# Down-projection of a streaming encoder layer: 38 of 44 k-tiles by one level of Strassen's algorithm, with sums of weights formed by accumulating transfers

## The chip, the core and the metric

The kernel runs on one core of one Trainium2 chip. The metric is the device time of one execution in microseconds (us). Before the change it is 2918.61 us, the median of 3 runs (2916.6 to 2919.67). The engines are TensorE (PE; its weight loads stand apart as PEld), VectorE (DVE), ScalarE (ACT), GpSimd (POOL) and SyncE (SP). SP issues nearly all transfers (queue q1), POOL the rest (queue q0); both queues run on the core's same 16 DMA engines.

## What is computed

One layer, 512 prompt frames and 64 sample frames together, model width 2048, FFN width 5632, float32:

```python
mod = jax.nn.silu(c) @ w_ada[l] + b_ada[l]
sh1, sc1, g1, sh2, sc2, g2 = jnp.split(mod[:, None, :], N_MOD, axis=-1)
h = rmsnorm(x, norm1[l]) * (1 + sc1) + sh1
mix, s_a, s_b, s_c = token_mixers(h, ...)      # w_in, two recurrences, w_out
x = x + g1 * mix
h = rmsnorm(x, norm2[l]) * (1 + sc2) + sh2
gate, val = jnp.split(h @ w_up, 2, axis=-1)
act = jax.nn.silu(causal_dwconv(gate, st, ffn_conv_w) + ffn_conv_b) * val
x = x + g2 * (act @ w_down)                    # the changed product, 5632 x 2048
y = rmsnorm(x, final_norm)
```

## The kernel before

**Tiling.** Activations lie as [128 features, 2 halves, 288 frames]: the 576 frames are cut into two halves of 256 prompt and 32 sample frames. Float32 products are made of three float32r products: each operand is split into a high part (ACT copies it, `hi`) and a rest (DVE subtracts, `lo`), and w·x is taken as hi·hi + hi·lo + lo·hi. So a product of a 128 x 128 weight block with both halves is 6 matmuls (`mm6`, L551: L560 four times, L562 twice). Weights come in pieces of 512 KB (`wtile`, L652, and `split`, L638: SP's load, ACT's copy L648, DVE's subtraction L649).

**Stages, in order of the program.** The head loads `w_ada` and forms the modulation `mod` on PE (L752, L756, L757), turns and normalises x (`x_turn`, `x_norm`) and starts on `w_in`; then come the heads of the two recurrences beside the products with `w_in`, `w_out`, the second norm, the up-projection (`up`, L1437), the down-projection (`down`, L1480) and the last four k-tiles with the final norm (`final`, L1511).

**POOL in the head.** POOL takes the reciprocal roots of five blocks of x (`rsqrt`, L143), clears four small tiles (`nar`, L867) and one more (`wg`, L953), and then begins the small triangular inverses of the first recurrence (`inverse16`, L346): it writes a matrix to DRAM (L355), reads blocks of it back (L361) and runs 28 short operations (L370, L371). What PE does with the inverse begins at L243.

**The up-projection** is by Strassen already: 44 output tiles t with 7 products each (`up_product`, L1362; 24 matmuls of 290 columns, hi·hi, hi·lo, lo·hi on one bank after the other), and sums of weights made by DVE (L1330, L1339, L1349, L1354). `steps` runs over (t, c), and `up_prep` splits two products ahead.

**The down-projection.** `down` loads the running sum x from DRAM (`xd`, 16 tiles), and for each of ten groups of four k-tiles goes over 16 output tiles m: 4 times `mm6` into a tile of PSUM, then `residual` (L1147, two DVE operations, L1150) adds g2 times that to x1[m]. Activations are loaded from DRAM (`actd`) and split ahead (`acts`, L1468). The eleventh group is done in `final`, half by half, and normalised as it goes.

**What sets the order.** The code is written in one order, and a scheduler puts each engine's instructions in an order of its own: an operation that waits for nothing that comes earlier in the code may be moved far ahead of its place, unless it is tied. An engine executes its list strictly in that order, and an instruction that waits for a semaphore holds up all that stand behind it. `high_priority` moves weight loads ahead by some 80 places.

Of the kernel before, what the change touches and what calls it, by code (L numbers as in the profile page):

```python
# [52 lines left out]
B11, T2, T1, B21, T3, B22, T4 = range(7)  # L53

# [46 lines left out]
class Kern:  # L101
# [530 lines left out]
    def raw_late(self):  # L632

        pool, tag = self.raws[self.n_raw % N_RAW]
        self.n_raw += 1
        return pool.tile([P, 1024], F32, tag=tag, name=self.name("raw"))
# [578 lines left out]
    def put(self, c, j, src, place=None):  # L1215

        place = place or self.places.pop(0)
        t = self.slot(place, F32R)
        self.split_z(t[:, 0], t[:, 1], src)
        self.combos[c, j] = t[:, 0], t[:, 1], place  # L1220
# [216 lines left out]
    def up(self):  # L1437
# [30 lines left out]
    def acts(self, g):  # L1468

        nc, out = self.nc, []  # L1470
        places = self.sets[g % 2]
        for n in range(4):
            raw, hh, hl = [self.slot(places[3 * n + i], (F32, F32R, F32R)[i], HT) for i in range(3)]
            nc.sync.dma_start(raw, self.actd[4 * g + n])
            nc.scalar.activation(hh, raw, AF.Copy)
            nc.vector.tensor_tensor(hl, raw, hh.bitcast(F32), op=ALU.subtract)
            out.append((hh, hl))
        return out

    def down(self):  # L1480
        free = [self.combos[c, j][2] for c in range(7) for j in range(NPAIR)]
        take = lambda n: [free.pop(0) for _ in range(n)]
        self.sets = [take(12), None]
        acts = self.acts(0)
        self.raw = self.raw_late
        places = take(KD)
        self.sets[1] = take(12)
        for m in range(KD):
            self.x1[m] = self.slot(places[m], F32)
            self.nc.sync.dma_start(self.x1[m], self.xd[m])  # L1490
        for g in range(NFF // 4 - 1):
            for m0 in range(0, KD, 2):
                wh, wl = self.wtile(self.w_down(4 * g, m0))
                if m0 == 6:
                    ahead = self.acts(g + 1)
                for m in range(m0, m0 + 2):
                    ps = self.pgt()
                    c = slice((m - m0) * P, (m - m0 + 1) * P)
# [3 lines left out]
            acts = ahead  # L1502
        g = NFF // 4 - 1
        self.final(acts, free + self.sets[(g + 1) % 2] + self.sets[g % 2][0::3])
# [5 lines left out]

    def final(self, acts, free):  # L1511
# [3 lines left out]

        wide = lambda n: [free.pop(0) for _ in range(n)]
# [5 lines left out]
        for h in range(2):  # L1522
# [3 lines left out]
            for m in range(KD):  # L1526
# [6 lines left out]
                self.residual(ps[:, m % 2:m % 2 + 1], self.x1[m][:, h:h + 1], self.mod[:, 5, m])  # L1533
# [40 lines left out]
    def final_part(self, h, q, blocks):  # L1574
# [3 lines left out]
        for c0, n, y, ms in blocks:  # L1578
            ps = self.bank()
            z0 = c0 if c0 < HP else ZS  # L1580
            for j in range(4):
                T.transpose(ps[:n, j * P:(j + 1) * P], self.x1[4 * q + j][:, h, z0:z0 + n], self.c["ident"])
# [23 lines left out]
def layer_kernel(tc, i, o):  # L1606
    nc = tc.nc
    with ExitStack() as ctx:
# [14 lines left out]
        K.actd = [dp.tile([P, 2, HT], F32, name=f"actd{t}") for t in range(NFF)]  # L1623
        K.hp = pool(ctx, "hp", bufs=1)
# [138 lines left out]
```

## Time and profile before

The profiled execution took 2917.59 us, of which 2915.8 us are the span from the first to the last instruction. Its clock was 0.994 of full speed.

| stage | from to, us | PE busy | DMA share |
|---|---|---|---|
| head, up to POOL's first L355 | 0 to 204.65 | 181.3 us | 0.92, 0.84, 0.94, 0.69 in its four parts |
| recurrences, w_in, w_out, norm | 204.65 to 1311.7 | 98 to 99% | about 0.55 |
| up-projection | 1311.7 to 2331.7 | 100% (1320 to 2310) | 0.36 |
| down-projection and final | 2331.7 to 2915.8 | 100% (2360 to 2800) | 0.33 (2360 to 2800) |

Of all DMA traffic (399.84 MB), 385.82 MB go by SP's queue and 10.68 MB by POOL's. "Busy" of PE is modelled from pipelined matmuls; the pace of matmuls is better read as a stretch of time over the number of matmuls begun in it. The DMA share is the mean share of time in which the 16 DMA engines work on a packet.

### The profile page before, as it was taken

What the parts mean: (1) busy time and instruction counts of PE and PEld (TensorE: products, weight loads), DVE (VectorE), ACT (ScalarE), POOL (GpSimd) and SP (SyncE); (2) the same over time, 40 slices, a digit from 0 to 9 for tenths busy, and PEclk for the clock granted to TensorE, in tenths of its full rate; (3) what the DMA queues carried; (4) which work ended last, traced back from release to release, by engine and by line L of the source; (5) the groups of instructions that cost most, each with busy time, mean ns of one, the idle gap of its engine ahead of it and who ended that gap; (6) DMA issues with size and microseconds to landing.
All of it is one profiled execution on the core that took longest, in us unless ns stands there. A gap on an engine that the chain in (4) does not pass through costs nothing.

```text
span 2915.8 us, 52420 instructions
## 1 busy us (share of the span) xinstructions
PE 2865.9 (98%) x21052; PEld 2766.4 (95%) x21052; DVE 2133.5 (73%) x3543; ACT 1239.9 (43%) x2118; POOL 321.0 (11%) x587
## 2 busy tenths in 40 slices
PE   7999999999999999999999999999999999999998
PEld 3599999999999999999999999999999999999997
DVE  5788878777777786468887888887888855555555
ACT  6574566544433233354444444444444422222223
POOL 0015432234210001000000000000000000000000
PEclk8999999999999999999999999999999999999999
DMA  8975555555456548333333333333333553333221
GB/s 302 302 205 148 157 154 159 155 140 165 124 149 174 145 144 250 113 104 106 107 100 105 106 107 106 107 99 106 105 106 107 175 185 102 114 102 113 87 81 66
DMA packets 511879, 399.84 MB, mean 137 GB/s; under 512 B 45865, under 2 KB 437764, under 8 KB 511636
## 3 DMA queue, kind: packets, MB, share of 16 engines
q1 hardware_dynamic: 506212, 385.82, 44.5%
q0 software_dynamic: 5424, 10.68, 1.1%
q8 instruction: 166, 2.72, 0.4%
q14 instruction: 77, 0.63, 0.1%
HBM read 356.27 MB, written 40.13 MB: 136 GB/s over the span
## 4 chain that ended last, share of the span: by engine, by line
PE 90%; DVE 4%; ACT 3%; DMA 2%; issue 1%; POOL 0%; SPq 0%; ACTq 0%; DVEq 0%; POOLq 0%
PE g L560 30%; PE g L562 15%; PE g L1372 9%; PE g L1373 8%; PE g L1374 8%; PE bank L1373 3%; PE bank L1372 3%; PE bank L1374 3%; PE bank L161 1%; DVE acc L819 1%; PE bank L825 1%; PE bank L433 1%; PE bank L752 1%; DVE wl L649 1%; PE bank L756 1%
## 5 line engine op out<-in xcount | busy, mean ns | idle before, releaser
L560 PE MATMUL g<-slot,wh 128*128 128x288 f32 x3168 | 551.4, 295 | 0.2 <-DVE slot L1150 0.2
L1372 PE MATMUL g<-slot,wh 128*128 128x290 f32 x1760 | 533.6, 303 | 3.0 <-ACT p L1384 2.6
L648 ACT ACTIVATE wh<-raw 128x1024 fp32r<-128x1024 f32 x239 | 253.0, 1059 | 658.5 <-PE g L560 622.5
L1373 PE MATMUL g<-slot,wh 128*128 128x290 f32 x1760 | 525.4, 299 | 0.0
L1374 PE MATMUL g<-slot,wl 128*128 128x290 f32 x1760 | 520.6, 296 | 0.0
L560 PEld LDWEIGHTS g<-slot,wh 128*128 128x128 f32 x3168 | 464.5, 188 | 0.7 <-DVE slot L1150 0.5
L560 PE MATMUL g<-hh,wh 128*128 128x288 f32 x1984 | 449.8, 306 | 2.3 <-ACT hh L1159 1.0
L560 PE MATMUL g<-hl,wh 128*128 128x288 f32 x1984 | 431.9, 297 | 0.0
L562 PE MATMUL g<-hh,wl 128*128 128x288 f32 x1984 | 431.5, 298 | 0.0
L1150 DVE SCALAR_TENSOR_TENSOR slot<-g,mod,slot 128x512 f32<-128x512 f32 (+1 forms) x448 | 201.8, 491 | 286.9 <-PE g L562 286.0
L1319 ACT ACTIVATE wh<-raw 128x1024 fp32r<-128x1024 f32 x176 | 186.8, 1061 | 390.2 <-PE g L1373 380.0
L1372 PEld LDWEIGHTS g<-slot,wh 128*128 128x128 f32 x1760 | 331.2, 188 | 17.6 <-ACT p L1384 11.7
L562 PE MATMUL g<-slot,wl 128*128 128x288 f32 x1584 | 341.7, 294 | 0.0
L1374 PEld LDWEIGHTS g<-slot,wl 128*128 128x128 f32 x1760 | 336.5, 191 | 0.0
L1373 PEld LDWEIGHTS g<-slot,wh 128*128 128x128 f32 x1760 | 335.6, 191 | 0.1
L649 DVE TENSOR_TENSOR wl<-raw,wh 128x1024 fp32r<-128x1024 f32 x239 | 291.4, 1220 | 52.2 <-ACT wh L648 51.3
L560 PEld LDWEIGHTS g<-hh,wh 128*128 128x128 f32 x1984 | 318.6, 190 | 5.5 <-ACT hh L1159 1.3
L560 PEld LDWEIGHTS g<-hl,wh 128*128 128x128 f32 x1984 | 320.9, 189 | 0.3
L562 PEld LDWEIGHTS g<-hh,wl 128*128 128x128 f32 x1984 | 319.4, 189 | 0.2 <-issue 0.2
L562 PEld LDWEIGHTS g<-slot,wl 128*128 128x128 f32 x1584 | 255.1, 188 | 0.0
L819 DVE SCALAR_TENSOR_TENSOR acc<-xr,ct,acc 128x512 f32<-128x512 f32 x322 | 230.3, 750 | 1.7 <-DMA xr<-in_w_ada_dram 1.7
L1320 DVE TENSOR_TENSOR wl<-raw,wh 128x1024 fp32r<-128x1024 f32 x176 | 214.7, 1220 | 18.3 <-ACT wh L1319 18.1
(373 smaller groups left out, 4540.5 us busy)
## 6 DMA issues: line engine op xcount, KB each, us to landing
raw<-in_w_up_dram SPq DMA_DIRECT2D x176, 512.0 KB
raw<-in_w_in_dram SPq DMA_DIRECT2D x108, 512.0 KB
raw<-in_w_down_dram SPq DMA_DIRECT2D x88, 512.0 KB
xr<-in_w_ada_dram SPq DMA_DIRECT2D x86, 512.0 KB
ax<-in_w_ada_dram SPq DMA_DIRECT2D x42, 512.0 KB
hraw<-in_w_ada_dram SPq DMA_DIRECT2D x40, 512.0 KB
raw<-in_w_out_dram SPq DMA_DIRECT2D x32, 512.0 KB
slot<-actd SPq DMA_DIRECT2D x44, 288.0 KB
```

The source lines that it names most:

```text
L161: self.nc.tensor.transpose(ps[:, b * P:(b + 1) * P], src4[:, b], self.c["ident"])
L560: T.matmul(ps[:, h if bank is None else bank, :n], wh, x[:, h, :n], start=f, stop=False)
L562: T.matmul(ps[:, h if bank is None else bank, :n], wl, ah[:, h, :n], start=False, stop=stop)
L648: nc.scalar.activation(hi[:, :n_], raw[:, :n_], AF.Copy)
L649: nc.vector.tensor_tensor(lo[:, :n_], raw[:, :n_], hi[:, :n_].bitcast(F32), op=ALU.subtract)
L819: V.scalar_tensor_tensor(acc[s], w[:, k], col, acc[s], op0=ALU.mult, op1=ALU.add)
L1150: self.nc.vector.scalar_tensor_tensor(x1[:, :, z], ps[:, :, c], gain[:, q:q + 1], x1[:, :, z], op0=ALU.mult, op1=ALU.add)
L1319: self.nc.scalar.activation(hi, src, AF.Copy)
L1320: self.nc.vector.tensor_tensor(lo, src, hi.bitcast(F32), op=ALU.subtract)
L1372: T.matmul(ps, wh[:, j], hi, start=(c < 3 and j == 0), stop=False, skip_group_check=True)
L1373: T.matmul(ps, wh[:, j], lo, start=False, stop=False, skip_group_check=True)
L1374: T.matmul(ps, wl[:, j], hi, start=False, stop=(j == NPAIR - 1), skip_group_check=True)
```

## The change

38 of the 44 k-tiles of the down-projection (2 to 39) are taken by one level of Strassen's algorithm. They form two halves of 19 (`NDOWN`), which with the two halves of the output width and the two halves of the frames make a 2 x 2 by 2 x 2 block product. Tiles 0 and 1 (`FIRST`) are done by `mm6` ahead of it, and 40 to 43 in `final` as before. The 19 pairs of k-tiles are cut into groups of 3, 4, 4, 4 and 4, and each group goes over four quarters q of the output half, with seven products c each; a product is 18 or 24 matmuls of 288 columns.

- `down_pair` makes the seven sums of activations of a pair of k-tiles and splits each (7 ACT copies, 7 DVE subtractions, 4 DVE sums). 
- `down_out` adds a finished product into one of 16 tiles of running sums (`acc`) or 4 of a common part (`e0`); `down_finish` puts a quarter together at the end: `e0`, times g2, plus x from DRAM. In `final`, `final_sum` takes the place of `residual`.
- The sums of weights are not made by DVE. `down_sums` has POOL issue 80 transfers from DRAM to DRAM: four copies and four accumulating transfers for each of 10 pieces, 72 of them of 256 rows by 1024 floats (1.05 MB) and 8 of half that. Each accumulating transfer waits for the landing of what it adds to. The generator is advanced twice in each of the first 40 rounds of the loop of the up-projection. `down_load` then loads weights and sums of weights alike, in 512 KB (384 KB in the first group).

```diff
+    def down_sums(self):
+        dma, add = self.nc.gpsimd.dma_start, ALU.add
+        pieces = [(g, k) for g in range(len(GROUPS)) for k in range(0, GROUPS[g], 2)]
+        for batch in (pieces[:5], pieces[5:]):
+            for op in range(8):
+                for g, k in batch:
+                    rows = slice(k * P, min(k + 2, GROUPS[g]) * P)
+                    a11, a12, a21, a22 = [self.down_block(g, *at)[rows] for at in ((0, 0), (0, 1), (1, 0), (1, 1))]
+                    s1, s2, s3, s4 = [w[rows] for w in self.ws[g]]
+                    to, of = ((s1, a21), (s1, a22), (s2, s1), (s2, a11), (s3, a11), (s3, a21), (s4, s2), (s4, a12))[op]
+                    if op % 2:
+                        dma(to, of, accum_op=add)
+                    else:
+                        dma(to, of)
+                    yield
     def up(self):
...
+        sums = self.down_sums()
         for n, (t, c) in enumerate(steps):
+            if c in (1, 4):
+                next(sums, None)
...
+    def down_product(self, step, c):
...
+        for a in range(2):
+            ps = self.banks[a][(0, 1, 2, 0, 1, 2, 1)[c]]
+            f = slice(a * P, (a + 1) * P)
+            for j in range(n):
+                hi, lo, _ = self.combos[c, j0 + j]
+                T.matmul(ps, wh[:, j, f], hi, start=(c < 3 and j == 0), stop=False, skip_group_check=True)
+                T.matmul(ps, wh[:, j, f], lo, start=False, stop=False, skip_group_check=True)
+                T.matmul(ps, wl[:, j, f], hi, start=False, stop=(j == n - 1), skip_group_check=True)
...
     def down(self):
...
-        for g in range(NFF // 4 - 1):
-            for m0 in range(0, KD, 2):
-                wh, wl = self.wtile(self.w_down(4 * g, m0))
...
-                    for k in range(4):
-                        self.mm6(ps, wh[:, k, c], wl[:, k, c], acts[k], k == 0, k == 3)
-                    self.residual(ps, self.x1[m], self.mod[:, 5, m])
...
+        steps = [((g, q), c) for g in range(len(GROUPS)) for q in range(4) for c in range(7)]
...
+        for n, (step, c) in enumerate(steps):
+            g, q = step
+            self.down_prep(n + 2)
+            self.down_product(step, c)
+            self.down_out(step, c)
...
+            if g < last and (q, c) in ((2, 0), (3, 1), (3, 3), (3, 5)):
...
+                self.down_pair(j, raws.pop(j))
+                j += 1
...
+        K.ws = [[dp.tile([n * P, D // 2], F32, name=f"ws{g}{c}") for c in range(4)] for g, n in enumerate(GROUPS)]
```

**Where the 80 transfers stand.** These are POOL's rows at the start of the program before the change (nar, rs and wg are the small tiles named above, d the matrix in DRAM that the first inverse writes):

```order
L867 MEMSET nar_777 128x264
L867 MEMSET nar_1055 128x264
L143 ISA
L143 TENSOR_TENSOR rs<-rs,mhalf 128x1 x4
L143 TENSOR_TENSOR rs<-rs,mhalf 64x1
L867 MEMSET nar_1333 128x264
L867 MEMSET nar_1456 128x264
L953 MEMSET wg 64x512
L355 DMA d_385_2078<-m_1867 128x512
L361 DMA m_1727<-d_385_2078 8x16x16 x4
```

And these are POOL's rows at the same place of the changed program (ws are the sums of weights in DRAM; L1543 is the copy, L1541 the accumulating transfer; all other lines stand two further down):

```order
L869 MEMSET nar_1075 128x264
L1543 DMA ws_177<-in_w_down_dram 256x1024
L1543 DMA ws_177<-in_w_down_dram 128x1024
L1543 DMA ws_181<-in_w_down_dram 256x1024 x2
L1543 DMA ws_185<-in_w_down_dram 256x1024
L1541 DMA ws_177<-in_w_down_dram 256x1024
L1541 DMA ws_177<-in_w_down_dram 128x1024
L1541 DMA ws_181<-in_w_down_dram 256x1024 x2
L1541 DMA ws_185<-in_w_down_dram 256x1024
L145 ISA
L145 TENSOR_TENSOR rs<-rs,mhalf 128x1
L1543 DMA ws_178<-ws_177 16x16384
```

Further on, still ahead of the first inverse, POOL's list of the changed program ends the transfers so:

```order
L869 MEMSET nar_1476 128x264
L1541 DMA ws_195<-in_w_down_dram 256x1024
L1543 DMA ws_188<-ws_186 16x16384
L1543 DMA ws_192<-ws_190 16x16384 x2
L1543 DMA ws_196<-ws_194 16x16384 x2
L1541 DMA ws_188<-in_w_down_dram 256x1024
L1541 DMA ws_192<-in_w_down_dram 256x1024 x2
L1541 DMA ws_196<-in_w_down_dram 256x1024 x2
L955 MEMSET wg 64x512
L357 DMA d_385_2098<-m_1887 128x512
```

All 80 transfers have moved from the loop of the up-projection, where the code has them, to the head: 24 stand ahead of the fifth root of x (L145), 49 ahead of the third `nar`, 69 ahead of the fourth, and the last eleven ahead of `wg` and the first inverse (L357). PE's and SP's lists are the same as before up to the end of the up-projection, ACT's but for one place, and DVE's but for a row or two moved by a few places.

**DVE where one group of pairs is followed by the next.** In the down-projection before the change DVE's list repeats this (L649 splits a weight piece, L1150 adds a product to x):

```order
L649 TENSOR_TENSOR wl_26503<-raw_26501,wh_26502 128x1024
L1150 SCALAR_TENSOR_TENSOR slot_25597<-g_26387,mod,slot_25597 128x2x256
L1150 SCALAR_TENSOR_TENSOR slot_25597<-g_26387,mod,slot_25597 128x2x32
L1150 SCALAR_TENSOR_TENSOR slot_25599<-g_26414,mod,slot_25599 128x2x256
L1150 SCALAR_TENSOR_TENSOR slot_25599<-g_26414,mod,slot_25599 128x2x32
```

In the changed program it has, in the last quarter of the second group (L1557 splits a weight piece, L1599 and L1601 add a product to the running sums, L1226 splits a sum of activations, L1501, L1505 and L1509 make such sums):

```order
L1557 TENSOR_TENSOR wl_27744<-raw_27582,wh_27743 128x1024
L1226 TENSOR_TENSOR slot_27780<-raw_27679,slot_27780 128x288
L1226 TENSOR_TENSOR slot_27786<-raw_27679,slot_27786 128x288
L1226 TENSOR_TENSOR slot_27789<-t_3691_27783,slot_27789 128x288
L1601 TENSOR_TENSOR slot_25672<-g_27619,slot_25672 128x576
L1226 TENSOR_TENSOR slot_27792<-raw_27681,slot_27792 128x288
L1226 TENSOR_TENSOR slot_27796<-raw_27681,slot_27796 128x288
L1509 SCALAR_TENSOR_TENSOR raw_27681<-raw_27679,raw_27681 128x288
L1557 TENSOR_TENSOR wl_27805<-raw_27613,wh_27804 128x1024
```

The work of `down_pair` now stands among the splits, spread over the twelve products around a change of group.

More of the change, by code (lines that the diff above doesn't have):

```diff
@@ L1465, in up, with stage @@
         self.up_act(t, self.v, self.ca)
[L1468 to L1478, printed above, removed]
+    def stage(self):
+        n = self.n_stage = self.n_stage + 1
+        tag = ("v", "cb", "v", "ca")[n % 4]
+        return self.ub.tile([P, 2, HZ], F32, tag=tag, bufs=2 if tag == "v" else 1, name=self.name("raw"))[:, :, :HT]
@@ new lines, in act_load, with act_split, pair_load @@
+    def act_load(self, t):
+        raw = self.stage()
+        self.nc.sync.dma_start(raw, self.actd[t])
+        return raw
+    def act_split(self, raw):
+        hh, hl = [self.slot(self.places.pop(0), F32R, HT) for _ in range(2)]
+        self.nc.scalar.activation(hh, raw, AF.Copy)
+        self.nc.vector.tensor_tensor(hl, raw, hh.bitcast(F32), op=ALU.subtract)
+        return hh, hl
+    def pair_load(self, j):
+        return [self.act_load(FIRST + j + half * NDOWN) for half in range(2)]
@@ L1503, in down @@
-        g = NFF // 4 - 1
-        self.final(acts, free + self.sets[(g + 1) % 2] + self.sets[g % 2][0::3])
+        self.raws += [(self.ua, "s1"), (self.ua, "s2")]
+        self.places = firsts = take(2 * FIRST)
+        firsts = list(firsts)
+        acts = [self.act_split(self.act_load(k)) for k in range(FIRST)]
+        self.places = take(7 * GROUPS[0])
+        quarters = lambda places: [self.slot(p, F32, HT) for p in places]
+        self.acc = {}
+        for row in range(2):
+            for h in range(2):
+                self.acc[row, h] = quarters(take(4))
@@ new lines, in down @@
+        self.e0_places = take(4)
+        self.e0 = quarters(self.e0_places)
+        self.places += free + firsts
+        self.g2 = self.sp.tile([P, KD, 2], F32, tag="g2", bufs=1, name="g2")
+        for half, f in ((0, 1.0), (1, -1.0)):
+            A.activation(self.g2[:, 8 * half:8 * half + 8], self.mod[:, 5, 8 * half:8 * half + 8], AF.Copy, scale=f)
+        steps = [((g, q), c) for g in range(len(GROUPS)) for q in range(4) for c in range(7)]
+        self.steps = steps
+        raws = {0: self.pair_load(0)}
```

155 lines of the change are left out of this document (136 added, 19 removed).

## The prediction

> **What bounds the kernel now.** I read the page's summary and its 40 slices first, then the busy time by stretches.
>
> ```profile
> span 2915.8 us, 52420 instructions
> PE 2865.9 (98%) x21052; PEld 2766.4 (95%) x21052; DVE 2133.5 (73%) x3543; ACT 1239.9 (43%) x2118; POOL 321.0 (11%) x587
> PE   7999999999999999999999999999999999999998
> DMA  8975555555456548333333333333333553333221
> ```
>
> PE is busy nearly everywhere, so fewer matmuls shorten the kernel wherever their weights and activations come in time. The DMA row says something else: it stands at 8, 9, 7 in the first three slices (0 to 219 us) and at 3 in the long middle. The stretches (columns: us, then busy us and count of PE, PEld, DVE, ACT, POOL, then PE's granted clock, DMA share, GB/s) give it in numbers:
>
> ```profile
> 0.00:50.00 50.00, 32.97 (x138) 19.87 (x139) 17.73 (x41) 35.17 (x75) 4.52 (x13) 0.84 0.92 312
> 50.00:100.00 50.00, 47.80 (x205) 24.26 (x204) 41.20 (x62) 30.13 (x44) 0.32 (x1) 0.99 0.84 281
> 100.00:150.00 50.00, 48.37 (x235) 28.69 (x234) 39.55 (x61) 27.24 (x37) 0.32 (x1) 1.00 0.94 317
> 150.00:204.65 54.65, 52.17 (x396) 51.07 (x395) 43.47 (x103) 41.56 (x93) 0.52 (x2) 1.00 0.69 193
> 125.00:150.00 25.00, 24.14 (x109) 13.00 (x108) 19.59 (x30) 13.26 (x19) 0.00 (x0) 1.00 0.95 318
> 1320.00:2310.00 990.00, 990.00 (x7218) 975.40 (x7217) 813.57 (x1005) 442.58 (x524) 68.17 (x129) 1.00 0.36 105
> 2360.00:2800.00 440.00, 440.00 (x3329) 440.00 (x3329) 234.09 (x383) 95.94 (x105) 0.00 (x0) 1.00 0.33 103
> ```
>
> So the head is bound by PE and DMA at once: its DMA engines have 0.92 × 50 + 0.84 × 50 + 0.94 × 50 + 0.69 × 54.65 = **172.7 us** of work in 204.65 us, and never show more than 0.95. The up- and down-projection have two thirds of the DMA time free.
>
> **The change, part by part.** *Matmuls.* By the code the last stage had 44 × 16 × 6 = 4224; now it has 6 × 16 × 6 = 576 and 19 × 4 × 2 × 7 × 3 = 3192, that is 456 fewer. The down-projection begins 3329 in 440 us, one in 132.2 ns: **60.3 us** less. But the new ones come in the order of the up-projection (hi·hi, hi·lo, lo·hi, one bank after the other), which begins 7218 of 290 columns in 990 us, one in 137.2 ns; at 288 columns 136.2, so 4.0 × 3192 = **12.9 us** back. (Some of that is waits of the up-projection alone; none of it would be the lower end.)
>
> *DVE in the new products.* Its rows in the trace of before:
>
> ```profile
> L649 DVE TENSOR_TENSOR wl<-raw,wh 128x1024 fp32r<-128x1024 f32 x83 | 101.0, 1217 | 0.9 <-ACT wh L648 0.8
> L1224 DVE TENSOR_TENSOR slot<-slot,slot 128x290 fp32r<-128x290 f32 x44 | 19.1, 456 | 8.3 <-ACT slot L1223 8.1
> L1397 DVE TENSOR_TENSOR g<-bank,g 128x290 f32<-128x290 f32 x44 | 20.1, 458 | 4.3 <-PE bank L1374 3.5
> L1476 DVE TENSOR_TENSOR slot<-slot,slot 128x576 fp32r<-128x576 f32 x44 | 33.1, 757 | 6.8 <-ACT slot L1475 6.2
> ```
>
> A product of 24 matmuls takes PE 3.27 us (24 × 136.2 ns); DVE spends on it a split (1.22) and an addition (0.8 for 576 columns, an estimate from the 757 ns of L1476), some 2.0 us, which lies beside PE. At a change of group four `down_pair`s come on top: twelve products there hold 12 splits, 9 additions of 576 and 6 of 288, 28 splits of a sum at 0.456 and 14 sums, together 44 us against 39 us of PE. Splits run two products ahead, which covers part; I take 2.5 us of waiting at each of four changes, 10 us. Where the first products begin, DVE has 31 us of splits and sums in front of it and PE 192 × 0.132 = 25 us of `FIRST`: 6 us. So the stage gains 60.3 − 12.9 − 16 = **31 us**; with all of it against me 5, with no stall and the old pace 60. The 320 operations of `residual` that go cost nothing before (DVE is busy 234 of 440 us), and gain nothing. The 140 loads of weights (80 before, so the share goes from 0.33 to some 0.6) are issued four products, 13 us, ahead and stay hidden.
>
> *The transfers.* The code has them in the up-projection; POOL's list has them in the head, ahead of everything that POOL does there (columns: start, us, what; in brackets the idle time before):
>
> ```profile
> 18.48 0.55 POOL L143 TENSOR_TENSOR rs<-rs,mhalf 128x1 f32<-128x1 f32 x1 [16.16 <-DVE rs L142]
> 48.86 0.54 POOL L143 TENSOR_TENSOR rs<-rs,mhalf 64x1 f32<-64x1 f32 x1 [9.02 <-DVE rs L142]
> 90.84 0.32 POOL L867 MEMSET nar<- 128x264 f32 x1 [41.44 <-PE g L876]
> 153.05 0.52 POOL L953 MEMSET wg<- 64x512 f32 x1 [31.35 <-DVE hl L585]
> 204.65 0.77 POOL L355 DMA_DIRECT2D d<-m  x1 [51.08 <-DVE m L1701]
> 208.74 2.43 POOL L361 DMA_DIRECT2D m<-d  x4 [3.32 <-DMA sd_k<-ts]
> ```
>
> All 80 must be issued, and the accumulating ones' destinations landed, before L355 of the first inverse. And PE cannot wait that out: in the chain of waits it reaches the first product with the inverse 48 us later,
>
> ```profile
> 252.74 0.84 PE bank L243 x8
> ```
>
> and its list is the old one. Issuing is cheap: 0.77 us for one, 2.43 for four, so 50 to 60 us of an idle POOL. Behind each waiting transfer stand the roots of x (and behind these DVE's and PE's scaling of x), `nar`, `wg` and the inverse.
>
> What the transfers cost the DMA engines no row shows; nothing in this kernel moves DRAM to DRAM or adds on the way. 8 × 19 pieces of 128 × 1024 × 4 bytes are 79.7 MB, half copied, half added. The price of a byte: the head moves 312 GB/s at 0.92, 339 at full share, mostly in rows of 2 KB; the up-projection 105 at 0.36, 292, in rows of 512 bytes. Four times the row is worth 1.16, so for rows of 4 KB an estimate of 394 at best. From below, every byte once at 394: 79.7 / 0.394 = **202 us** of all 16 engines. From above, each end in DRAM paid as a pass of its own (two for a copy, three for an addition): 5 × 39.85 / 0.394 = **506 us**. I take a copy as one pass and an addition, which must read two streams, as two, at 366, between 339 and 394: 3 × 39.85 / 0.366 = **327 us**. Nothing excludes either end.
>
> The Trainium skill (Collectives: The Full Stack, "The bandwidth ceiling: the fold count and why AG ≠ RS ≠ AR") states that an addition inside a transfer needs two source reads on one ring and runs at half the rate of a copy. No run here shows it; by it the term stays, and without it the cheap rival below holds.
>
> *What that delays.* The engines then have 327 + 172.7 us of work before POOL and PE stand where they stood at 204.65. At the 0.95 that is the most the head shows, (327 + 172.7) / 0.95 = 526 us, a delay of **321 us**. Hardly any is taken back: a queue that is served in turn with the transfers starves, so PE gets its weights later, and after the head PE is 98 to 100% busy.
>
> Sum, against the profiled execution (2917.59 us, 1 us below the median): 2917.6 + 321 − 31 = 3208, or **3209 us** by the median.
>
> **The rivals.** *Dear transfers.* 506 us of work: (506 + 172.7) / 0.95 − 204.65 = 510, so 3397 us (3422 with the small gain). For it: DRAM is at both ends. Against it: no row shows DRAM as the limit. The Trainium skill (DMA: Bandwidth & Descriptors, "Latency and other measured facts") gives 214 GB/s for copies between tensors in device memory; by that, with twice for additions, the work would be an estimated 558 us and the time 3452. No run here shows it.
>
> *Cheap transfers.* An addition costs what a copy does, 202 us: (202 + 172.7) / 0.95 − 204.65 = 190, so 3078 us (3050 with the full gain).
>
> *Faster after all: the transfers run beside the loads.* If POOL's queue takes nothing from SP's, the loads come as before, and only POOL's list counts: the first inverse is late by what the transfers take beyond 204.65 us. With 202 us that is nothing, and the time 2918 − 31 = 2887; with 327 it is 122 and 3009. It turns to slower at 204.65 + 31 = 236 us, that is when 79.7 MB run at under 338 GB/s beside loads that run at 300. For it: POOL's queue is its own. Against it: the share stops at 0.95, and the busiest stretch has 318 GB/s; both together would need twice that.
>
> *The change not doing what it says* is contained above: the sums are not made in the stage ahead of the down-projection. Made there, with 0.64 of 1009 us free, they would be hidden and the time 2887; POOL's list excludes it.
>
> **How the numbers follow.** Forecast (an addition as two passes) 0.48, dear 0.25, cheap 0.17, beside the loads 0.10, half of it faster. The range goes from 3040, a little under the cheap case with its full gain, to 3420, the dear case with a small one; it leaves out what is dearer still and the case beside. Faster by over 0.2% (what a measurement of this kernel can tell from no change) 0.05, within it 0.01, slower 0.94.
>
> **What would show it.** In the changed profile: POOL's first inverse (L357) begins near 525 us instead of 204.65, with waits for ws transfers ahead of it; the DMA share is 9 in the slices up to there, and q0 carries 90 MB; PE shows long waits for `w_ada` and `w_in`; the up-projection takes 1010 to 1020 us as before; from its end to the end of the kernel are some 553 us instead of 584. I am wrong if L357 starts near 205 us, if SP's loads land as fast beside the transfers as without them, or if the last stage isn't shorter.

## The result, and the profile after

| | before | after |
|---|---|---|
| median of the runs | 2917.61 us (2916.59 to 2919.67, 4 runs) | 3162.25 us (3160.36 to 3165.26, 4 runs) |
| ratio, 95% interval | | 1.0838 (1.082 to 1.0857) |
| first inverse on POOL begins | 204.65 us | 497.07 us |
| up-projection, first to last matmul | 1311.7 to 2331.5, 1019.8 us | 1603.5 to 2622.2, 1018.7 us |
| from there to the end of the span | 584.3 us | 539.5 us |

The kernel is slower by 245 us. The table says where: the first inverse is 292.4 us later, the up-projection is as long as before (1.1 us less), and what follows it is 44.8 us shorter. 292.4 − 1.1 − 44.8 = 246.5; the spans differ by 245.9.

Of the changed kernel's page, the summary, the slices (79 us each) and POOL's DMA queue (packets, MB, share of 16 engines' span):

```profile
span 3161.7 us, 52259 instructions
PE 2859.3 (90%) x20596; PEld 2725.6 (86%) x20596; DVE 2228.5 (70%) x3662; ACT 1358.9 (43%) x2379; POOL 373.2 (12%) x667
PE   3334379999999999999999999999999999999997
PEclk7556589999999999999999999999999999999999
DMA  9999986445555454665333333333333335666671
...
q0 software_dynamic: 21616, 90.37, 10.9%
```

The loss stands in the first five or six slices: DMA is at 9 there, PE at 3 and 4. POOL's queue q0 carries 90.37 MB (10.68 before). In stretches of 100 us (columns as in the prediction):

```profile
0.00:100.00 100.00, 30.25 (x108) 16.43 (x108) 15.40 (x34) 31.61 (x63) 20.61 (x36) 0.69 1.02 286
100.00:200.00 100.00, 35.75 (x87) 13.28 (x87) 18.97 (x31) 16.75 (x29) 15.16 (x22) 0.59 1.04 288
200.00:300.00 100.00, 52.59 (x171) 25.93 (x172) 32.81 (x49) 22.21 (x29) 13.79 (x20) 0.67 1.01 294
300.00:400.00 100.00, 28.86 (x102) 17.58 (x100) 14.95 (x23) 11.53 (x17) 12.11 (x17) 0.59 1.04 274
400.00:500.00 100.00, 86.10 (x525) 69.51 (x526) 64.06 (x133) 56.82 (x114) 1.13 (x2) 0.88 0.80 224
```

DMA's share is 1.01 to 1.04 for 400 us (it adds up the durations of both queues' packets, and can pass 1) and PE works 29 to 53 of each 100 us: the head has become bound by DMA alone. Four rows of the waits of the first 500 us (sum, count, longest) show on whom it falls:

```profile
ACT wh L650 <- DMA hraw<-in_w_ada_dram: 135.0, 21, 15.4
PE bank L754 <- DMA raw<-in_w_ada_dram: 101.3, 6, 37.5
POOL ws L1541 <- DMA ws<-in_w_down_dram: 88.2, 16, 23.7
POOL ws L1541 <- DMA ws<-ws: 62.5, 15, 22.2
```

PE and ACT wait for `w_ada`, and POOL for its own transfers. POOL's timeline shows that the transfers are over long before the inverse begins:

```profile
387.07 0.87 POOL L1541 DMA_DIRECT2D ws<-in_w_down_dram  x1 [2.96 <-DMA ws<-ws]
445.40 0.52 POOL L955 MEMSET wg<- 64x512 f32 x1 [57.46 <-DVE hl L587]
497.07 0.61 POOL L357 DMA_DIRECT2D d<-m  x1 [51.15 <-DVE m L1900]
```

The last transfer is issued at 387; POOL then waits 57 us for DVE (`hl`) and 51 us for DVE (`m`); before the change these two waits were 31 and 51 us. What is late there is the data, not POOL. The chain of work that ended last says the same (start, us, what): up to the first inverse some 314 us of it are landings of SP's loads, 20 us before the change, and no instruction of POOL stands in it. Two of its pieces:

```profile
333.56 35.07 DMA hraw<-in_w_ada_dram
375.19 45.05 DMA hraw<-in_w_ada_dram
```

The DMA queues up to the first inverse (packets, MB, share of the stretch), in the changed kernel from 0 to 497.07 us and in the kernel before from 0 to 204.65:

```profile
q0 software_dynamic: 16192, 79.70, 62.9%
q1 hardware_dynamic: 44947, 55.88, 35.3%
```

```profile
q1 hardware_dynamic: 44944, 55.87, 83.9%
```

The loads ahead of the first inverse are the same, and they take the engines as long: 0.353 × 497.07 = 175 us, before 0.839 × 204.65 = 172. What is new is the transfers' work, 0.629 × 497.07 = 313 us.

The last part, before and after, cut where the old products with `mm6` end and where the new products begin and end:

```profile
2331.50:2839.50 508.00, 508.00 (x3844) 507.99 (x3843) 276.07 (x452) 115.39 (x130) 0.00 (x0) 1.00 0.35 113
2839.50:2915.80 76.30, 63.71 (x484) 61.41 (x481) 45.06 (x119) 24.79 (x63) 3.18 (x6) 0.95 0.18 64
```

```profile
2622.20:2657.40 35.20, 27.95 (x195) 27.39 (x194) 27.69 (x63) 26.17 (x71) 0.15 (x2) 0.90 0.56 170
2657.40:3080.40 423.00, 422.85 (x3194) 422.64 (x3193) 341.72 (x508) 204.37 (x311) 0.00 (x0) 1.00 0.65 200
3080.40:3161.70 81.30, 65.37 (x484) 62.85 (x483) 48.79 (x125) 28.58 (x73) 3.18 (x6) 0.91 0.19 67
```

The 3192 new products take 423.0 us, one in 132.5 ns, and PE has no gap at a change of group.

### The profile page after: what moved, and what is told of

It reads as the page before. It is cut to its first block, busy times and chain, and to the rows that moved or that the text cites. A ratio compares the mean times of both kernels' runs of the same rounds, so it can differ in the third digit from the quotient of the medians.

```text
span 3161.7 us, 52259 instructions
## 1 busy us (share of the span) xinstructions
PE 2859.3 (90%) x20596; PEld 2725.6 (86%) x20596; DVE 2228.5 (70%) x3662; ACT 1358.9 (43%) x2379; POOL 373.2 (12%) x667
## 3 DMA queue, kind: packets, MB, share of 16 engines
q0 software_dynamic: 21616, 90.37, 10.9%
## 4 chain that ended last, share of the span: by engine, by line
PE 78%; DMA 12%; DVE 5%; ACT 3%; SPq 1%; issue 1%; another core or an unknown queue 1%; POOL 0%; ACTq 0%; DVEq 0%; POOLq 0%
PE g L562 17%; PE g L564 8%; PE g L1374 8%; PE g L1375 8%; PE g L1376 7%; DMA hraw<-in_w_ada_dram 4%; PE bank L1375 3%; PE bank L1374 3%; PE g L1584 3%; PE bank L1376 3%; PE g L1586 3%; PE g L1585 3%; DMA raw<-in_w_ada_dram 2%; DMA hs<-in_x_prompt_dram 1%; PE bank L1584 1%; PE bank L1585 1%
## 5 line engine op out<-in xcount | busy, mean ns | idle before, releaser
L1321 ACT ACTIVATE wh<-raw 128x1024 fp32r<-128x1024 f32 x176 | 186.7, 1061 | 395.4 <-PE g L1375 387.9
L650 ACT ACTIVATE wh<-raw 128x1024 fp32r<-128x1024 f32 x163 | 172.6, 1059 | 410.2 <-PE g L562 276.6
L1374 PEld LDWEIGHTS g<-slot,wh 128*128 128x128 f32 x1760 | 331.0, 188 | 16.7 <-ACT p L1386 11.3
L1376 PEld LDWEIGHTS g<-slot,wl 128*128 128x128 f32 x1760 | 336.3, 191 | 0.0
L1375 PEld LDWEIGHTS g<-slot,wh 128*128 128x128 f32 x1760 | 334.8, 190 | 0.1
L651 DVE TENSOR_TENSOR wl<-raw,wh 128x1024 fp32r<-128x1024 f32 x163 | 198.9, 1221 | 153.9 <-ACT wh L650 153.3
L1322 DVE TENSOR_TENSOR wl<-raw,wh 128x1024 fp32r<-128x1024 f32 x176 | 214.7, 1220 | 18.8 <-ACT wh L1321 18.6
L1584 PE MATMUL g<-slot,wh 128*128 128x288 f32 x760 | 224.3, 295 | 0.1
L1586 PE MATMUL g<-slot,wl 128*128 128x288 f32 x760 | 223.9, 295 | 0.0
L1585 PE MATMUL g<-slot,wh 128*128 128x288 f32 x760 | 223.8, 295 | 0.0
L1556 ACT ACTIVATE wh<-raw 128x1024 fp32r<-128x1024 f32 (+1 forms) x140 | 142.1, 1015 | 171.9 <-PE g L1585 100.3
L1375 PE MATMUL bank<-slot,wh 128*128 128x290 f32 x704 | 210.1, 298 | 0.0
```

The source lines that it names most:

```text
L651: nc.vector.tensor_tensor(lo[:, :n_], raw[:, :n_], hi[:, :n_].bitcast(F32), op=ALU.subtract)
L1321: self.nc.scalar.activation(hi, src, AF.Copy)
L1322: self.nc.vector.tensor_tensor(lo, src, hi.bitcast(F32), op=ALU.subtract)
L1374: T.matmul(ps, wh[:, j], hi, start=(c < 3 and j == 0), stop=False, skip_group_check=True)
L1375: T.matmul(ps, wh[:, j], lo, start=False, stop=False, skip_group_check=True)
L1376: T.matmul(ps, wl[:, j], hi, start=False, stop=(j == NPAIR - 1), skip_group_check=True)
```

## The experiments

Each time stands beside runs of the kernel before on the same chip (medians 2916.8 to 2918.7 us). "Up-projection" is the stretch from its first to its last matmul.

| kernel | first inverse | up-projection | time, us | ratio to before (95%) |
|---|---|---|---|---|
| e3, transfers alone | 498.3 | 1020.8 | 3215.55 | 1.1017 (1.1002 to 1.1032) |
| e4, copies for additions | 416.1 | 1019.3 | 3086.29, one run | |
| e8, copies to places of their own | 412.8 | 1018.4 | 3074.28, one run | |
| e12, short transfers | 208.4 | 1019.2 | 2875.80 | 0.9848 (0.9827 to 0.9868) |
| e2, no transfers | 204.7 | 1018.6 | 2869.20 | 0.9838 (0.9826 to 0.9851) |
| e1, tied | 202.3 | 1063.6 | 2917.84 | 1.0003 (0.9993 to 1.0014) |
| e7, mixed | 201.4 | 1063.7 | 2914.82 | 0.9994 (0.9984 to 1.0005) |
| e6, behind a split | 203.4 | 1033.3 | 2885.92 | 0.9898 (0.9879 to 0.9917) |
| e9, e6 with the addition first | 206.6 | 1030.6 | 2884.76 | 0.9884 (0.9867 to 0.9901) |
| e11, parted | 203.6 | 1106.0 | 2961.26 | 1.0147 (1.013 to 1.0163) |
| e5, behind the sum at a11 | 202.3 | 1365.9 | 3226.95 | 1.1057 (1.1031 to 1.1083) |
| e10, e5 in small packets | 207.0 | 1438.7 | 3295.90 | 1.1298 (1.1282 to 1.1313) |

### Is it the transfers, and is it their work?

**e3** puts the 80 transfers into the kernel before, which keeps its old down-projection.

```diff
 # the kernel before
+        sums = self.down_sums()
         for n, (t, c) in enumerate(steps):
+            if c in (1, 4):
+                next(sums, None)
```

> The kernel before, with its old down-projection, plus the 80 transfers alone, whose sums nobody reads; POOL's list has them in the head as in the changed kernel. Theory: the whole loss is the transfers', and independent of the new products: 2918 + 292 = 3210 us, first inverse near 497 us. Rival (the head is late for another reason, such as SP's loads reordered by the new last stage): well below 3210.

Measured: 3215.55 us. POOL's timeline (its L356 is L357 of the changed kernel):

```profile
498.31 0.61 POOL L356 DMA_DIRECT2D d<-m  x1 [50.48 <-DVE m L1732]
```

The loss is the transfers' alone, 298 us here. **e2** is the counterpart.

```diff
 # the changed kernel
-            if c in (1, 4):
-                next(sums, None)
...
-        src = (self.down_block(g, 0, 0), s2, s1, self.down_block(g, 0, 1), s3, s4, self.down_block(g, 1, 1))[c]
+        src = self.down_block(g, *((0, 0), (1, 0), (1, 1), (0, 1), (0, 0), (1, 0), (1, 1))[c])
```

> The new down-projection without any of the 80 transfers; it reads blocks of w_down where it read sums, so its output leaves the sums of weights out. Theory: the head is that of before (first inverse near 205 us), and the end of the up-projection to the end of the kernel is 539 us as in the changed kernel: 2873 us, ratio 0.985. What lies between this and the tied transfers is the price of hidden transfers. Rival (part of the 45 us came from a shift of work, such as loads of the last stage done ahead while PE starved): the stage is longer than 539 us and the time above 2885.

Measured: 2869.20 us, 538.3 us behind the up-projection. So the new products are worth 48 us (1.6%), and nothing of that came from loads done ahead in a starved head. Together, e2 and e3 split the change in two: about −48 and +298 us.

**e4** keeps POOL's list and its waits, and makes every addition a copy.

```diff
                     if op % 2:
-                        dma(to, of, accum_op=add)
+                        dma(to, of)
```

> The changed kernel with the 40 accumulating transfers turned into plain copies of the same size, at the same places and with the same waits; the additions of weights are left out. Theory (DMA work): an accumulating packet of 4 KB takes 327 ns and a copied one 159, so the 40 additions cost 100 us less, the transfers 210 instead of 312 us, and the first inverse begins at (210 + 172.7)/0.975 = 393 us, 104 us earlier: 3058 us. Rival (POOL's waits from landing to landing set the delay, not the amount of work): POOL has the same 80 in the same chain, and the first inverse stays above 450 us, the time above 3110.

```profile
416.13 0.59 POOL L357 DMA_DIRECT2D d<-m  x1 [50.56 <-DVE m L1900]
```

The first inverse is 81 us earlier (expected 104). The time, 3086 us, lies 28 us above the theory's 3058 and 24 us below the rival's 3110: by itself not clear. **e8** was to take POOL's waits away.

```diff
-                    s1, s2, s3, s4 = [w[rows] for w in self.ws[g]]
-                    to, of = ((s1, a21), (s1, a22), (s2, s1), (s2, a11), (s3, a11), (s3, a21), (s4, s2), (s4, a12))[op]
-                    if op % 2:
-                        dma(to, of, accum_op=add)
-                    else:
-                        dma(to, of)
+                    to = self.ws[g][op][rows]
+                    of = (a21, a22, a12, a11, a11, a21, a22, a12)[op]
+                    dma(to, of)
...
```

> The changed kernel with 80 plain copies of blocks of w_down, each to a place of its own, so that POOL waits for no landing between them; the additions of weights are left out. The copies stand at the same places of POOL's list, in the head. Theory (the head is late because the engines have the transfers' work to do): 80 copies at 159 ns for 4 KB are 193 us of work, (193 + 172.7)/0.975 - 204.65 = 170 us of delay, 2869 + 170 = 3040 us, although POOL has issued all within some 120 us. Rival (POOL's waits from landing to landing make the head late): without them the first inverse begins near 205 to 230 us and the time is under 2900.

```profile
312.86 0.55 POOL L1540 DMA_DIRECT2D ws<-in_w_down_dram  x1 [3.17 <-DMA ws<-in_w_down_dram]
412.75 0.59 POOL L357 DMA_DIRECT2D d<-m  x1 [51.49 <-DMA m<-gd]
```

3074 us, by the numbers the theory's side. But the edit did not do what it was meant to: POOL still waited 39 times, 129.2 us in all, for earlier transfers to land, though none touched another's data, and issued the last at 312.86 us instead of within 120. So e8 does not part work from waits. What both kernels have less of is work: up to their first inverse the transfers take 217 us of the engines in e4 (0.522 × 416.13) and 220 in e8 (0.533 × 412.75) in place of 313, beside 171 us of the same loads; the two queues' shares add up to 0.93 and 0.95 there. **e12** comes from the other end: all 80 transfers with their places and waits, and about a fifteenth of the bytes.

```diff
 # with e2's edit of down_load
-                    rows = slice(k * P, min(k + 2, GROUPS[g]) * P)
+                    rows = slice(k * P, k * P + 16)
```

> The changed kernel with all 80 transfers at their places in POOL's list, each with the same waits, but of 16 rows in place of 256 or 128 (64 KB, 5.2 MB in all in place of 79.7); the down-projection reads blocks of w_down where it read sums, so the sums of weights are left out. Theory (the head is late because the engines have the transfers' work to do): the work is about 20 us, the first inverse begins at 205 to 230 us, and the time is 2870 to 2900 us. Rival (the transfers that POOL must issue and wait for, ahead of the roots, nar and the inverse, hold up the head whatever their size): 80 issues of 0.55 to 0.9 us and about 30 waits for a landing of 2 to 3 us are 130 us, and the first inverse begins above 300 us, the time near 3000.

Measured: 2875.80 us. Of the groups of POOL's instructions up to 215 us the transfers (busy, mean ns, idle before them), and the first inverse in its timeline:

```profile
L1541 POOL DMA_DIRECT2D ws<-in_w_down_dram x40 | 31.7, 1156 | 17.4 <-DMA ws<-in_w_down_dram 9.6 <-DMA ws<-ws 7.8
L1543 POOL DMA_DIRECT2D ws<-in_w_down_dram x20 | 12.1, 874 | 0.2 <-issue 0.2
L1543 POOL DMA_DIRECT2D ws<-ws x20 | 10.7, 681 | 3.3 <-DMA ws<-in_w_down_dram 3.3
```

```profile
208.44 0.62 POOL L357 DMA_DIRECT2D d<-m  x1 [50.87 <-DVE m L1900]
```

POOL still issues all 80 in the head (54.5 us of issuing, some 21 us of waiting), and the first inverse is 3.8 us late. The 80 places and their waits, which are short here because a short transfer lands soon, cost at most 4 to 7 us; the other 290 come with the bytes. In the changed kernel POOL waits 191 us for landings, but not on the chain that sets the time, as shown above.

### Are they hidden in the up-projection?

The prediction gave 2887 us for sums "made there", because 0.64 of the up-projection's DMA time is free. **e1** makes them there.

```diff
             if c in (1, 4):
-                next(sums, None)
+                if t > 0:
+                    with self.tc.issue_after(self.pool_of):   # POOL's last copy into fs
+                        next(sums, None)
```

> The 80 transfers are tied behind POOL's copies of the same round of the up-projection (tiles 1 to 40), so POOL's list in the head is that of before. Theory (the 292 us are the transfers' 312 us of DMA work done in a head that has no DMA time free): the first inverse begins near 205 us again, the up-projection has 0.64 x 1020 = 650 us of DMA time free, the 312 us disappear in it, and only the 45 us won behind the up-projection are left: 2918 - 45 = 2873 us, DMA share in the up-projection 0.36 + 312/1020 = 0.67. Rival (packets of the two queues take turns, so that a 4-KB transfer packet of 159 or 327 ns stands between any two of the up-projection's short weight packets): the up-projection is starved while a transfer runs and grows by 50 us or more, 2920 us or above.

Measured: 2917.84 us, just under the rival's 2920: the 48 us are lost again, 45 of them in an up-projection with DMA time to spare (share 0.71 from 1400 to 2300 us). The waits from 1300 to 2400 us, in the kernel before, in e2 and in e1 (L1339 and L1341 are the sum that needs `a11`):

```profile
DVE s L1339 <- DMA raw<-in_w_up_dram: 46.3, 42, 1.6
```

```profile
DVE s L1341 <- DMA raw<-in_w_up_dram: 41.6, 42, 1.6
```

```profile
DVE s L1341 <- DMA raw<-in_w_up_dram: 97.1, 42, 6.2
```

Read the first row again: before any change, each of 42 tiles already waits 1.1 us for that load. There are six buffers; each load is issued the moment its buffer is free and lands when DVE is already there. Such a load has no slack, however idle the DMA engines. By the distance of the tiles' first matmuls, most tiles of e1 with two copies last 23.0 us, as in e2; those with two additions up to 29.6.

I took it that the transfers only had to miss `a11`, and made two kernels, **e5** meant to be good and **e6** meant to be bad; in both a tile has one copy and one addition.

```diff
+    def sums_after(self, src):
+        self.nc.gpsimd.tensor_copy(self.probe, src)
+        with self.tc.issue_after(self.nc.cur_bb.bb.instructions[-1]):
+            next(self.weight_sums, None)
...
             V.tensor_tensor(s2, g("s1"), g("a11"), op=ALU.subtract)
+            if t > 0:
+                self.sums_after(s2[:, 0, 0:1])                       # e5
...
             w = self.up_split(g("a22"))
+            self.sums_after(w[1][:, 0, 0:1].bitcast(F32))            # e6
```

> The transfers in the up-projection, but one copy and one addition in each tile (in place of two of a kind), and POOL issues them behind a one-column copy of the sum that DVE makes at L1341, so that they start when the tile's a11 has landed. Theory (the 44 us of the tied kernel are late landings of a22 and a11: each w_up load is issued the moment its buffer is free and lands about 1 us after DVE could have used it, so whatever transfers add to it is lost; two additions keep the engines 10 to 13 us, into the next tile's a22 and a11): from a11's landing to the next a22 are 16 us of the 23 us of a tile, the two transfers (about 10 us beside the loads of a12 and a21, which have time) fit in, and the time is that without transfers, 2869 to 2880 us, faster than the kernel before by 1.3 to 1.6%. Rival (the up-projection pays for the amount of transfer work, wherever in the tile it lies): the 44 us stay, 2910 to 2920.

> The same as the timed kernel with one edit: POOL's transfers of a tile start behind the split of the tile's last product (the moment at which the load of a22 gets its buffer), so that they run beside the loads of a22 and a11. Theory (late a11): a11 lands 3 to 4 us later in each of 40 tiles, the up-projection grows by 100 to 160 us, 2970 to 3030 us. Rival (amount of work): as the tied kernel, 2918.

Both fell, the other way round: e5 3226.95 us, e6 2885.92, faster than the kernel before by 1.0%. One tile of e5 in the timeline (SP's row at 1715.42 begins with the load of `a12`, L1363 is the sum that needs it):

```profile
1715.38 0.51 POOL L1549 DMA_DIRECT2D ws<-ws  x1
1715.42 3.01 SPq L1320 DMA_DIRECT2D raw<-in_w_up_dram  x2
1715.87 0.92 POOL L1547 DMA_DIRECT2D ws<-in_w_down_dram  x1
1729.43 1.23 DVE L1363 TENSOR_TENSOR s<-raw,s 128x1024 f32<-128x1024 f32 x1 [9.07 <-DMA raw<-in_w_up_dram]
```

And of e6 (L1361 is the same sum):

```profile
1709.34 3.01 SPq L1320 DMA_DIRECT2D raw<-in_w_up_dram  x2
1710.43 0.51 POOL L1548 DMA_DIRECT2D ws<-ws  x1
1710.92 0.93 POOL L1546 DMA_DIRECT2D ws<-in_w_down_dram  x1
1714.17 1.23 DVE L1361 TENSOR_TENSOR s<-raw,s 128x1024 f32<-128x1024 f32 x1
```

In e5 POOL issues its two transfers within 0.5 us of `a12`'s load, and DVE gets `a12` 14.0 us after it was issued. In e6 POOL issues them 1.1 and 1.6 us after it; `a12` is used after 4.8 us, without a wait. My reading of the loads was wrong: the two without slack are `a11` and `a12`, while `a21` and `a22` are loaded a tile ahead, and e6's release comes by luck when most of `a12` is through. In e5 the release hangs on DVE's L1346, and `a12`'s buffer on the split that DVE does right behind it, so that nearly every tile is hit: most last 33 to 35 us.

What happens on the engines is in the DMA view of e5 from 1721 to 1725.5 us (packets, MB, share):

```profile
q0 software_dynamic: 186, 0.76, 94.8%
q1 hardware_dynamic: 184, 0.09, 10.4%
```

The two queues are served one packet for one, although the packets hold so different amounts: 184 short ones of the load (512 bytes) get 0.10 of the time, 186 of the addition (4 KB) 0.95. A load whose row is short thus has to sit out nearly the whole transfer beside it.

**e7** releases the same pairs at e1's place.

```diff
+            if t > 0 and c == 1:
+                with self.tc.issue_after(self.pool_of):
+                    next(self.weight_sums, None)                     # one copy and one addition
```

> One copy and one addition in each tile as in the timed kernel, but released as in the tied one, behind POOL's copies into fs, some 4 us later than the timed kernel's. Theory: the transfers run from about 13 to 23 us of the tile, and just touch the next a22 but hardly a11: most of the 44 us come back, 2875 to 2895 us. Rival (amount of work): 2918.

```profile
DVE s L1341 <- DMA raw<-in_w_up_dram: 110.2, 42, 5.3
```

2914.82 us, near the rival's 2918: hardly better than e1. The same transfers thus cost 45 us, 15 us or 347 us of up-projection by the moment of their release alone (e7, e6, e5, against 1018.6 us). **e9** turns e6's pair round.

```diff
-            for op, (g, k) in [s for s in slot if s]:
+            for op, (g, k) in [s for s in slot[::-1] if s]:
```

> The kernel of e6 with the two transfers of a tile in the other order: the addition first, then the copy. In e6 the tiles that carry an addition and a copy in 4-KB packets end their transfers about 21 us into the tile and last 23.0 to 25.0 us, where a tile without any lasts 23.0: the tail meets the loads of a22 and a11. Theory (packets of the two queues that both wait are served one for one, so a load beside a copy pays 159 ns a packet, and beside an addition 327): a tail of copy packets delays those loads half as much, and about half of the 15 us lost in the up-projection come back: 2875 to 2882 us. Rival (only the end of the transfers counts, not what they are): 2886 as e6.

2884.76 us: the rival; the up-projection is still 12 us longer than without transfers (15 in e6). **e10** shortens the packets of e5.

```diff
+                to, of = [w.rearrange("p (c n) -> c p n", c=8) for w in (to, of)]
                 if op % 2:
                     dma(to, of, accum_op=add)
```

> The kernel of e5, where each tile lasts some 34 us because a12's load meets the transfers, with every transfer written as rows of 128 floats, so that its packets are 512 bytes as those of the loads. Theory (one packet for one): a load has 64 packets on each engine, and each now waits for a short packet (an estimate of 27 ns for a copy, 54 for an addition, from the 512-byte loads' 27 and the ratio 327 to 159) in place of 159 or 327 ns: a12 is late by 2 to 4 us a tile in place of 11, the loss in the up-projection 80 to 160 us in place of 358, 2950 to 3030 us, although the queue of transfers has more work. Rival (the transfers go first, or bytes are shared out evenly): the loss grows with the transfers' work, 3230 us or above.

3295.90 us, a miss. The additions went out in 512-byte packets, but the copies in 4 KB, and a short addition packet took 65 ns, not 54, so that q0 worked much longer:

```profile
q0 software_dynamic: 181808, 91.31, 16.1%
```

0.161 × 3296 = 531 us, against 0.117 × 3212 = 376 in e5. Here `a11` came late too: DVE waits for it at L1358, 172.3 us in 39 tiles from 1400 to 2700 us, and DVE's list has another order than in e5 (L1358 stands right ahead of L1363). So e10 differs from e5 in more than its packets, and neither supports nor refutes the turns of the queues; it shows that packets made small in this way are no way out. **e11** releases copy and addition apart.

```diff
 # e6, with a step of the generator for each transfer
+            if t + 1 < NFF:
+                self.sums_after(self.a[t + 1, "a11"][:, 0, 0:1])
             V.tensor_tensor(g("s2"), g("a12"), g("s2"), op=ALU.subtract)
```

> As e6, but the two transfers of a tile are released apart: the copy behind the landing of a11 (POOL copies one column of it), the addition as in e6 some 3 us later, when a12's load is already on its way. The trace of e6 shows the loads that cannot wait, a11 and a12 (a21 and a22 are loaded a tile ahead), with about 5 us between a11's landing and a12's first packet, and 13 us between a12's landing and the next a11. Theory (only what meets a11 or a12 costs): the copy (2.5 us) goes into the first gap, the addition into the second, which is no longer filled to its end, and most of the 15 us that e6 loses in the up-projection come back: 2870 to 2880 us. Rival (the copy does not fit, since a transfer begins about 1.5 us after it is issued): its tail meets a12 as in e5, a12 lands up to 3 us later in each tile, 2900 us or above.

```profile
1690.00 1.23 DVE L1346 TENSOR_TENSOR s<-s,raw 128x1024 f32<-128x1024 f32 x1 [1.19 <-DMA raw<-in_w_up_dram]
1691.21 0.51 POOL L1554 DMA_DIRECT2D ws<-ws  x1
1692.39 3.06 SPq L1320 DMA_DIRECT2D raw<-in_w_up_dram  x2
1698.57 1.23 DVE L1363 TENSOR_TENSOR s<-raw,s 128x1024 f32<-128x1024 f32 x1 [1.36 <-DMA raw<-in_w_up_dram]
```

2961.26 us, the rival. The gap that I had read as 5 us is smaller: `a12`'s load is issued 2.4 us after `a11` is in use, the copy 1.2 us before it, and so the copy meets `a12`: in the waits that sum (L1363) has 96.4 us over 39 tiles, up to 9.6.

## Why the prediction was right, and where it was not

**POOL's list and the shared engines: right.** The forecast rested on two readings: all 80 transfers stand in the head, and the head has no DMA time to give. The change costs about what the transfers work, 292 us against 321 forecast; e12 shows that the list with little of the work costs 4.

**The price of an addition: right.** It was taken as two passes, a copy as one. In the records of q0 a 4-KB packet of a copy takes 159 ns and one of an addition 327; the transfers together are 312 us of the 16 engines, against 327. The cheap rival (an addition as dear as a copy, 3078 us) is nearly what e4 built, 3086. The Trainium skill (Collectives: The Full Stack, "The bandwidth ceiling: the fold count and why AG ≠ RS ≠ AR") has an addition, in rings of cores, at half a copy's rate; 327 against 159 ns agrees. The Trainium skill's 214 GB/s for copies, a figure for rows of 16 KB issued by other engines (DMA: Bandwidth & Descriptors, "Latency and other measured facts"), by which 3452 us would have come out, was too low here: 16 packets of 4096 bytes in 159 ns are 412 GB/s, and the measurement decides.

**The rest of the delay was mis-sized.** The prediction's sum took 0.95, the most that the head had shown, as the share that the engines reach; in the same terms it was (312 + 172.7) / 497.07 = 0.975. This 0.975 is worked out from the measured 497 us, so it says how large the term was and is no check of the sum; e4 and e8 came to 0.93 and 0.95. Of the 29 us of difference to 321, 16 come from the work and 13 from the share.

**"Beside the loads": refuted.** That rival needed POOL's queue to take nothing from SP's. From 100 to 200 us of the changed kernel:

```profile
q0 software_dynamic: 4237, 20.34, 79.1%
q1 hardware_dynamic: 4457, 8.47, 25.3%
```

4457 packets of loads for 4237 of transfers, one for one, and a quarter of the time for a queue that had most of it. The Trainium skill (DMA: Bandwidth & Descriptors, "Queues, rings and completion order") says that each engine takes turns between its queues by packets; these counts agree. By the Trainium skill such a packet holds typically 9 to 17 descriptors; the records here count one for one down to single rows of 512 bytes (e5), and the measurement decides. Turns between queues of unequal packets are what the forecast's "starves" comes to.

**The last stage: 45 us instead of 31; of its terms only the count of matmuls held.** The step "the new ones come in the order of the up-projection, which begins one in 137.2 ns" charged 12.9 us for the order; the new products run at 132.5 ns, 1 us more than `mm6` at 132.2. The up-projection's pace contains waits of its own (139 of the 7214 distances between its matmuls from 1320 to 2310 us are over 180 ns, none of those in the old down-projection), which the prediction named and did not follow. The step "2.5 us of waiting at each of four changes" was 0: DVE is busy 341.7 of 423.0 us, but splits that run two products ahead cover the burst. (Four `down_pair`s are 16 sums, not 14; that changed nothing.) The 6 us at the first products came out by luck. The step "DVE has 31 us of splits and sums in front of it and PE 192 × 0.132 = 25 us" would have PE wait for DVE at the end of `FIRST`, and there it does not wait: the new products follow without a gap. Its 6.0 us lie ahead of `FIRST`, where it waits for ACT's copy of the activations, which have just been loaded:

```profile
PE g L562 <- ACT slot L1488: 6.0, 1, 6.0
```

Around it are 3.7 us more (35.2 us for 193 matmuls that take 25.5), and `final` is 5.0 us longer (81.3 against 76.3), which the prediction did not have: 2.7 of them are a wait of PE for DVE's last sums (L1780 for L1707) that was not there before, and the rest is not explained. 60.3 − 1 − 9.7 − 5.0 = 44.6.

**"Made there, with 0.64 of 1009 us free, they would be hidden": wrong.** This side remark was the weakest step. It took a mean share for slack. Two of the four loads of each tile of the up-projection have none, and by the moment of release the same transfers cost 15 to 347 us (e6, e5). Its 2887 us were met by e6, at 2885.92, but not for that reason: e1, which does what the code says, is at 2917.84.

**Open.** What loses the last 12 to 15 us of e9 and e6 was not settled to the end. In e6 it is again the sum that needs `a11`:

```profile
DVE s L1346 <- DMA raw<-in_w_up_dram: 71.6, 42, 3.9
```

That is 30 us more than in e2. By the distance of the tiles' first matmuls, 14 of the 15 us stand in 13 of the tiles, which last 23.1 to 25.0 us; in these the copy is issued 19.3 to 21.2 us after the tile's first matmul, in the others, which last 23.0, after 18.0 to 19.2. So the moment decides here too; what shifts it from tile to tile is open. Nor was it tried whether a stage whose loads have slack would take the transfers free.

## What to carry to other kernels

See in each engine's own order where a transfer without inputs ends up: the line in the code does not hold it, and a busy stage at the start is where it lands. The free share of the DMA engines is no room for more transfers as long as the stage's loads are issued when their buffer comes free: look for a wait of 1 us on each load, and ask when in the loop a transfer would meet one. Where it must, tie its release to an event of that loop and try several: here one release gave 1.0% less than before, another 10.6% more.

## What the runs showed of the hardware that was not expected

- Two queues with work share an engine packet by packet, not byte by byte: 184 packets of 512 bytes beside 186 of 4 KB, at 0.10 and 0.95 of the time (e5); 4457 beside 4237 in the changed kernel's head.
- An accumulating packet from DRAM to DRAM takes 327 ns for 4 KB where a copy takes 159, and 65 ns for 512 bytes where a load to the chip takes 27 (e10). The copies from one sum to the next (16x16384 in POOL's list) go in packets of 64 KB, some 2.8 us each; from 154 to 168 us of the changed kernel, where 64 of them begin, both queues still count 214 packets, at 0.97 and 0.10 of the time.
- POOL waited 39 times for landings of transfers that shared no data with the next (e8); from where this comes was not looked into.
- The granted clock in PE's rows was 0.59 to 0.69 for 400 us of the starved head, where it was 0.84 to 1.00 before and 0.93 to 1.00 in e12. PE had 29 to 53 us of work in 100 there, so it cannot be said that the clock cost anything.
